# Conditioning products of a two-layer diffusion step: float32 weights stationary on TensorE, the two condition vectors moving

## The chip, the core and the metric

The kernel is one program on one core of a Trainium2 chip. The core has TensorE (matrix products; the profile shows its products as PE and its weight loads as PEld), VectorE (DVE), ScalarE (ACT), GpSimd (POOL), and SyncE (SP), which issues the DMAs. Each engine works through its own list of instructions in order. The metric is the device time of one execution in microseconds; lower is better. Three runs of the kernel before took 1280.70, 1283.64 and 1284.29 us, the median is 1283.64.

## What is computed

One inference step of a network of two layers for 1024 latent tokens and 256 context tokens, 1024 channels, float32. Layer 0 has two attention mixers, layer 1 a Fourier mixer. Ahead of each layer its tokens are normalised, scaled and shifted, and behind it its output is multiplied by a gate. Shift, scale and gate are linear in a conditioning vector; there are two such vectors, `c` for the latent tokens and `c_ctx` for the context. Only these products change. In the reference:

```python
def ada_mod(cvec, w, b):
    m = jax.nn.silu(cvec) @ w + b
    return jnp.split(m, 3, axis=-1)

def modulate(h, shift, scale):
    return h * (1 + scale) + shift
...
    for l in range(DEPTH):
        shc, scc, gtc = ada_mod(c_ctx, ada_w[l], ada_b[l])
        shl, scl, gtl = ada_mod(c, ada_w[l], ada_b[l])
        hc = modulate(rms_norm(xc, norm_g[l]), shc, scc)
        hl = modulate(rms_norm(xl, norm_g[l]), shl[:, None], scl[:, None])
        ...
        xc = xc + gtc * yc
        xl = xl + gtl[:, None] * yl
```

`ada_w[l]` has 1024 rows and 3072 columns: part 0 is the shift, part 1 the scale, part 2 the gate, 1024 columns each. So there are six products, one for each layer and part, of two vectors of 1024 with a matrix of 1024 x 1024.

## The kernel before

Large products run on TensorE in a float32 form (`F32R`) that takes one pass and keeps fewer bits. To keep the precision, an operand is split into a high and a low half (`split`: the high half is a copy, the low half a subtraction), and a product is made of three matmuls, high x high, high x low and low x high (`mm3`, line 249). A matmul's stationary operand is loaded as weights, 128 x 128 at most, and the other operand streams past it.

Buffers come from zones of fixed tiles (`take` and `drop`): `w` has 8 tiles, `p` 4, `pt` 3, `q` 2, `h` 9, `u` 26. A tile is taken again when its last reader is done. The tile framework puts the instructions of each engine in an order of its own when the program is built, so an engine's order isn't that of the code.

The program's stages, with the times of the profiled execution:

- **The first stage** (to 83 us): a fold product (`wa`, line 249), normalising the first 512 tokens, and a loop over 8 chunks `k` of 128 channels. For a chunk, `ada_load` loads two tiles of `ada_w` (parts 0 and 1 of layer 0; 8 blocks of 128 rows by 128 columns, 512 KB), and `ada_chunk` makes shift and scale of these 128 channels. It splits each tile into two halves (lines 261 and 267, on ACT, DVE and POOL) and makes the two condition vectors stationary: `cs4` holds their high and low halves, 4 columns. The tile's halves stream past as 128 columns (lines 491 and 493, `ada`). The result has 4 rows; ACT copies it, and a small plain float32 matmul with `comb` (line 499, `modt`) adds the halves and turns rows into columns. `mod_chunk` makes the modulated chunk, and the projections that need it run (`kv0s`, `kv2s`, `q0s`, `q2s`, line 510).
- **The list `S1`** (83 to 141 us): the other tokens are normalised and modulated (`xt`, line 413, transposes), and keys, values and queries are projected (`kv`, `q`, line 249), normalised, rotated and transposed (`kT`, `qT`, line 646). The letters of `S1` are steps: `n` normalise, `m` modulate, `c` cache, `k`, `q`, `K`, `Q` projections.
- **The attention of mixers A and B** (141 to about 865 us). `soft` makes scores (`sL`, `sC`, line 840) and their exponentials, `weigh` transposes these (`pt`, line 957) and multiplies with the values (`av`, line 963). Between these units a `Filler` runs other work from a queue by cost: projections of the order `ORDER`, and ahead of the first four work items of `qb0`, `qb1` and `g0` the steps named in `COND`: the products (layer 0, part 2), (1, 0) and (1, 1). A step (`Rows.step_ap`) loads 128 rows of a part (512 KB), multiplies them by the first vector's elements and adds on DVE (line 351, two halves), and does the same for the second vector with ACT (line 355) and POOL (line 356). After 8 steps `Rows.finish` splits the two sums and adds their 128 rows with a matmul against ones (line 365), and `row_to_mod` turns the row into columns by 8 small transposes (line 309); the gate's row is stored to memory.
- **Output projection of layer 0** (`oz`), to about 945 us.
- **Layer 1** (from 945 us): gate products (`g1E`, `g1O`, `g1c`), between them the sixth product (1, 2) on DVE alone (`Rows.step`, line 339), the Fourier products and the last projection (`of`).

The lines that the change replaces are 309, 335 to 383 (`Rows`) and 479 to 504.

Of the kernel before, what the change touches and what calls it, by code (L numbers as in the profile page):

```python
# [30 lines left out]
S1 = "c1 n2 m1 c0 m2 K0 Q0 Q2 K2 k6 q8 k4 k8".split()  # L31
E_ML = ("p", "d")
E_MF, E_MH, LC0 = "da", "d", "ppd"
E_AH, E_AL = "a", "dpp"
# [17 lines left out]
COND = ("qb0", "qb1", "g0")  # L52
# [70 lines left out]
def hybrid_step(ctx: ExitStack, tc: tile.TileContext, I, O):  # L123
# [35 lines left out]
    def t_bank(name, dt=F32):  # L159
        return bank("t", name, dt)  # L160
# [34 lines left out]
    cs4 = cp.tile([P, 8, 4], F32R, name="cs4")  # L195
    comb = cp.tile([4, 2], F32, name="comb")
    bT1 = cp.tile([P, 8], F32, name="bT1")
    gT = cp.tile([P, 2, 8], F32, name="gT")
    bT = cp.tile([P, 2, 16], F32, name="bT")
# [17 lines left out]
    dve.tensor_copy(cs4[:, :, 0:2], cs)  # L217
    dve.tensor_sub(cs4[:, :, 2:4], cs, cs4[:, :, 0:2])
    dve.tensor_add(comb, ident[0:4, 0:2], ident[0:4, 2:4])
# [86 lines left out]
    def row_to_mod(l, part, row):  # L306
        tp = t_bank(f"modt{l}{part}")
        for k in range(8):
            pe.transpose(tp[:, 2 * k : 2 * k + 2], row[0:2, k * P : k * P + P], ident[0:2, 0:2])
        tv = tp[:, 0:16].rearrange("p (k v) -> p k v", v=2)  # L310
        bb = bT[:, l, 8 * part : 8 * part + 8].unsqueeze(2).to_broadcast([P, 8, 2])
        if part == 0:
            dve.tensor_add(modb[:, l], tv, bb)
        else:
# [4 lines left out]
    def ada_src(l, part, k):  # L319
        return I["ada_w"][l, k * P : (k + 1) * P, part * D : (part + 1) * D]  # L320

    class Rows:
        def __init__(self, l, part, name, tags):
            self.l, self.part, self.name, self.tags = l, part, name, tags
            self.acc = [take(tags, (P, D)) for v in range(2)]
            for a in self.acc:
                pool.memset(a.a, 0.0)
                if part == 2:
                    sp.dma_start(a[0:1, :], I["ada_b"][l : l + 1, 2 * D : 3 * D])

        def step(self, k, wt=None):
            own = wt is None
            if own:
                wt = take(self.tags, (P, D))
                sp.dma_start(wt.a, ada_src(self.l, self.part, k))
            for v in range(2):
                for h in range(2):
                    sl = slice(h * 512, h * 512 + 512)
                    dve.scalar_tensor_tensor(
                        out=self.acc[v][:, sl], in0=wt[:, sl], scalar=cs[:, k, v : v + 1], in1=self.acc[v][:, sl],  # L340
                        op0=ALU.mult, op1=ALU.add,
                    )
            if own:
                drop(wt)

        def step_ap(self, k):
            wt = take(self.tags, (P, D))
            sp.dma_start(wt.a, ada_src(self.l, self.part, k))
            for h in range(2):
                sl = slice(h * 512, h * 512 + 512)  # L350
                dve.scalar_tensor_tensor(  # L351
                    out=self.acc[0][:, sl], in0=wt[:, sl], scalar=cs[:, k, 0:1], in1=self.acc[0][:, sl],
                    op0=ALU.mult, op1=ALU.add,
                )
            act.activation(wt.a, wt.a, AF.Copy, scale=cs[:, k, 1:2])  # L355
            pool.tensor_add(self.acc[1].a, self.acc[1].a, wt.a)  # L356
            drop(wt)

        def half(self, h, ps, start=True, stop=True):
            for v in range(2):  # L360
                src = self.acc[v][:, h * 512 : h * 512 + 512]
                hi, lo = take("h", (P, 512), F32R), take("h", (P, 512), F32R)
                split(hi.a, lo.a, src)
                for i, part in enumerate((hi, lo)):
                    pe.matmul(
                        ps[0:2, :], ones2[:, v, :], part.a, start=start and v + i == 0, stop=stop and v + i == 2
                    )
                drop(hi, lo)

        def total(self, ps, start=True, stop=True):  # L370
            for h in range(2):
                self.half(h, ps[h], start, stop)
            drop(*self.acc)

        def finish(self, tag):
            row = take(self.tags, (P, D))
            for h in range(2):
                ps = bank(tag, f"{self.name}p{h}")
                self.half(h, ps)
                act.activation(row[0:2, h * 512 : h * 512 + 512], ps[0:2, :], AF.Copy)  # L380
            drop(*self.acc)
            if self.part == 2:
                sp.dma_start(gtd[self.l], row[0:2, :])
            else:
                row_to_mod(self.l, self.part, row.a)
            drop(row)
# [87 lines left out]
    def ada_load(k):  # L474
        out = []
        for part in range(2):
            raw = take(("p", "pt", "q"), (P, 8, P))
            c0 = part * D + k * P
            sp.dma_start(raw.a, I["ada_w"][0, :, c0 : c0 + P].rearrange("(b p) c -> p b c", p=P))
            out.append(raw)  # L480
        return out

    def ada_chunk(k, raws):
        ps = bank("g", f"ada{k}")
        for part, raw in enumerate(raws):
            hi, lo = take("u", (P, 8, P), F32R), take("u", (P, 8, P), F32R)
            split(hi.a, lo.a, raw.a, E_AH, E_AL)
            drop(raw)
            out = ps[0:4, part * P : part * P + P]
            for b in range(8):  # L490
                pe.matmul(out, cs4[:, b, :], hi[:, b, :], start=b == 0, stop=False)
            for b in range(8):
                pe.matmul(out[0:2], cs4[:, b, 0:2], lo[:, b, :], start=False, stop=b == 7)
            drop(hi, lo)
# [3 lines left out]
        for part in range(2):  # L498
            pe.matmul(
                tp[:, 2 * part : 2 * part + 2], row[:, part * P : part * P + P], comb, start=part == 0, stop=part == 1  # L500
            )
        drop(row)
        dve.tensor_scalar(modb[:, 0, k, :], tp[:, 0:2], bT[:, 0, k : k + 1], None, op0=ALU.add)
        dve.tensor_scalar(moda[:, 0, k, :], tp[:, 2:4], bT1[:, k : k + 1], gT[:, 0, k : k + 1], op0=ALU.add, op1=ALU.mult)
# [322 lines left out]
    drop_w(wka)  # L827
    ws["qa1"] = load_w(w0cols(C_QA + 256))
# [181 lines left out]
    cond = dict(zip(COND, ((0, 2), (1, 0), (1, 1))))  # L1010
    rows, wout = {}, []
# [11 lines left out]
    def releaser(nm):  # L1023
        def fn():
            drop_w(ws[nm])
            return 0
        return fn

    def cond_steps(key, ks):
        def fn():  # L1030
            if key not in rows:
                rows[key] = Rows(*key, f"ad{key[0]}{key[1]}", "w")
            for k in ks:
                rows[key].step_ap(k)
            if ks[-1] == 7:
                rows[key].finish("g")
            return 0
        return fn

    for i, nm in enumerate(order):  # L1040
# [302 lines left out]
    r2 = Rows(1, 2, "ad12", BIG)  # L1343
    for c in range(4):
# [43 lines left out]
        for k in ((), (0, 1, 2), (3, 4, 5), (6, 7))[c]:  # L1388
            r2.step(k)
# [4 lines left out]
    r2.finish("g")  # L1394
# [434 lines left out]
```

## Time and profile before

| | us |
|---|---|
| median of 3 runs | 1283.64 |
| the profiled execution | 1282.65 |
| its span, first to last instruction | 1280.9 |
| PE busy in it | 1191.8 |
| DVE / ACT / POOL busy | 955.5 / 639.3 / 489.1 |

The page lists each engine's busy time, then the span in 40 slices of 32 us. A busy PE is not yet PE at its peak: each matmul's record includes its latency, while the next one has already started. What a matmul costs in a stream is the distance from its start to the next one's, its pitch. `PEclk` is the clock that the throttle granted to TensorE, in tenths of full speed. The chain of waits follows the work that ended last back to the start and names TensorE for 62% of the span, DVE for 15%.

### The profile page before, as it was taken

What the parts mean: (1) busy time and instruction counts of PE and PEld (TensorE: products, weight loads), DVE (VectorE), ACT (ScalarE), POOL (GpSimd) and SP (SyncE); (2) the same over time, 40 slices, a digit from 0 to 9 for tenths busy, and PEclk for the clock granted to TensorE, in tenths of its full rate; (3) what the DMA queues carried; (4) which work ended last, traced back from release to release, by engine and by line L of the source; (5) the groups of instructions that cost most, each with busy time, mean ns of one, the idle gap of its engine ahead of it and who ended that gap; (6) DMA issues with size and microseconds to landing.
All of it is one profiled execution on the core that took longest, in us unless ns stands there. A gap on an engine that the chain in (4) does not pass through costs nothing.

```text
span 1280.9 us, 21997 instructions
## 1 busy us (share of the span) xinstructions
PE 1191.8 (93%) x7883; PEld 1066.0 (83%) x7883; DVE 955.5 (75%) x2114; ACT 639.3 (50%) x1239; POOL 489.1 (38%) x386
## 2 busy tenths in 40 slices
PE   5789899999889899999999978889999998999997
PEld 5788899999879798889999977767777888988886
DVE  6789788776987987977887867466874988548553
ACT  5363366565675576756655677431264324333221
POOL 6757665522775754530101042310411215335001
PEclk8898899999999999999999989889999999999999
DMA  9900332324634336344433388596412544346321
GB/s 303 290 6 31 110 90 71 98 68 107 188 110 134 103 122 177 112 138 129 105 90 87 95 241 223 135 253 202 138 59 75 158 154 142 101 140 191 124 90 66
DMA packets 156199, 168.29 MB, mean 131 GB/s; under 512 B 21917, under 2 KB 117161, under 8 KB 156090
## 3 DMA queue, kind: packets, MB, share of 16 engines
q1 hardware_dynamic: 156090, 166.89, 44.4%
q8 instruction: 62, 1.02, 0.4%
q14 instruction: 47, 0.39, 0.1%
HBM read 122.67 MB, written 44.18 MB: 130 GB/s over the span
## 4 chain that ended last, share of the span: by engine, by line
PE 62%; DVE 15%; DMA 11%; issue 5%; POOL 4%; ACT 3%; SPq 1%; POOLq 0%; DVEq 0%; ACTq 0%
PE ga L249 7%; PE of L249 7%; PE av L963 7%; PE pt L957 6%; PE oz L249 5%; PE q L249 4%; PE u L249 4%; PE g1E L249 4%; PE sL L840 3%; PE g1O L249 2%; DVE w L351 2%; PE kv L249 2%; PE sC L840 2%; DVE p L874 2%; DMA od<-e 2%
## 5 line engine op out<-in xcount | busy, mean ns | idle before, releaser
L960 DVE TENSOR_TENSOR pt<-pt,pt 128x512 fp32r<-128x512 f32 (+1 forms) x264 | 171.1, 658 | 34.5 <-ACT pt L261 34.1
L963 PE MATMUL av<-pt,u 128*128 128x256 f32 x1008 | 171.0, 292 | 7.4 <-DVE pt L960 4.0
L261 ACT ACTIVATE pt<-pt 128x512 fp32r<-128x512 f32 (+1 forms) x264 | 146.9, 574 | 60.8 <-PE pt L957 36.4
L957 PE MATMUL pt<-identr,p 128*128 128x128 f32 x1008 | 156.6, 274 | 0.7 <-ACT h L261 0.5
L963 PEld LDWEIGHTS av<-pt,u 128*128 128x128 f32 x1008 | 142.0, 192 | 16.6 <-DVE pt L960 7.1
L267 POOL TENSOR_TENSOR w<-h,w 128x512 fp32r<-128x512 f32 x58 | 79.6, 1384 | 180.6 <-ACT w L261 78.7
L249 PE MATMUL q<-w,u 128*128 128x256 f32 x864 | 132.3, 294 | 1.8 <-DVE u L438 1.0
L957 PEld LDWEIGHTS pt<-identr,p 128*128 128x128 f32 x1008 | 119.7, 141 | 9.5 <-ACT h L261 0.9
L249 PE MATMUL ga<-u,w 128*128 128x512 f32 (+1 forms) x576 | 123.5, 360 | 0.1
L881 ACT ACTIVATE p<-p,nm 128x1280 f32<-128x1280 f32 (+1 forms) x80 | 95.3, 1192 | 54.7 <-DVE p L874 54.3
L249 PEld LDWEIGHTS q<-w,u 128*128 128x128 f32 x864 | 117.1, 195 | 6.1 <-DVE u L438 1.8
L249 PEld LDWEIGHTS ga<-u,w 128*128 128x128 f32 x576 | 93.7, 188 | 15.0 <-ACT pt L261 0.6
L840 PE MATMUL sL<-u,q 128*128 128x512 f32 x256 | 85.2, 418 | 11.6 <-DVE p L874 8.5
L249 PE MATMUL oz<-u,w 128*128 128x512 f32 x240 | 68.5, 413 | 9.8 <-ACT w L261 9.8
L356 POOL TENSOR_TENSOR w<-w,w 128x1024 f32<-128x1024 f32 x24 | 58.6, 2442 | 43.9 <-ACT w L355 33.4
L881 ACT ACTIVATE p<-p,NM 128x640 f32<-128x640 f32 (+2 forms) x80 | 59.2, 740 | 32.4 <-DVE p L874 32.2
L840 PE MATMUL sC<-u,q 128*128 128x256 f32 x320 | 63.2, 300 | 9.4 <-DMA q<-qd 5.8
L249 PE MATMUL of<-u,u 128*128 128x512 f32 (+1 forms) x219 | 65.8, 388 | 0.0
L249 PEld LDWEIGHTS oz<-u,w 128*128 128x128 f32 x240 | 45.9, 196 | 20.0 <-ACT w L261 10.4
L874 DVE TENSOR_SCALAR_CACHE_REDUCE p<-sC,nsink 128x256 f32<-128x256 f32 x80 | 37.8, 475 | 30.3 <-PE sC L840 25.6
L840 PEld LDWEIGHTS sC<-u,q 128*128 128x128 f32 x320 | 48.9, 192 | 13.4 <-issue 5.8
L249 PE MATMUL kv<-w,u 128*128 128x256 f32 x384 | 56.2, 290 | 0.0
(773 smaller groups left out, 2881.8 us busy)
## 6 DMA issues: line engine op xcount, KB each, us to landing
q<-qd SPq DMA_DIRECT2D x80, 256.0 KB
w<-i_ada_w SPq DMA_DIRECT2D x24, 512.0 KB
h<-i_w_in SPq DMA_DIRECT2D x40, 256.0 KB
qd<-h SPq DMA_DIRECT2D x40, 256.0 KB
h<-i_w_out SPq DMA_DIRECT2D x32, 256.0 KB
h<-i_wuT SPq DMA_DIRECT2D x16, 256.0 KB
u<-i_x SPq DMA_DIRECT2D x8, 512.0 KB
p<-i_ada_w SPq DMA_DIRECT2D x8, 512.0 KB
```

Of the source, the lines that this page charges most:

```text
L249: pe.matmul(out, a, b, start=i == 0, stop=i == n - 1)
L261: act.activation(out, in_, AF.Copy)
L267: pick("lo" + lc, lc).tensor_sub(dst_l, src, dst_h)
L351: dve.scalar_tensor_tensor(out=self.acc[0][:, sl], in0=wt[:, sl], scalar=cs[:, k, 0:1], in1=self.acc[0][:, sl], op0=ALU.mult, op1=ALU.add,)
L356: pool.tensor_add(self.acc[1].a, self.acc[1].a, wt.a)
L840: pe.matmul(ps, q[:, s, hc * P : hc * P + P], keys, start=s == 0, stop=s == 1)
L874: dve.tensor_scalar(p[i][:, end[i] : end[i] + n], ps, sign, last[i], op0=ALU.mult, op1=ALU.min, accum_out=c)
L881: act.activation(p[i][:, 0 : end[i]], p[i][:, 0 : end[i]], AF.Exp, bias=last[i], scale=-1.0, accum_out=SU[:, t, hd + i, 0:1],)
L957: pe.transpose(tp[:, jj * 256 + i * P : jj * 256 + i * P + P], p[i][:, off : off + P], ident)
L960: dve.tensor_sub(pt[:, 1, 0:n], tp[:, 0:n], pt[:, 0, 0:n])
L963: pe.matmul(acc, vv, pt[:, s, jj * 256 : jj * 256 + 256], start=c + jj + s == 0, stop=c + jj == nt - 1 and s == 1,)
```

## The change

All six products take one form. A tile of `ada_w` (8 blocks of 128 x 128, as in `ada_load`) is loaded for each chunk of 128 columns, and each block is the stationary operand of a plain float32 matmul, unsplit; the moving operand is `cs`, the two vectors, two columns wide. The result stands as columns already, so the split of the weights, the copy, `comb` and the transposes of shift and scale go. The first layer's shift and scale stay in the loop of the first stage. The other four products, 32 tiles, are put between the steps of `S1` by the table `AT_N`: no tile ahead of the first two steps, two ahead of each of the next four, three ahead of each of four, and four ahead of the last three. The gate's columns become rows by one transpose and are stored at the end of `S1`. `Rows`, `row_to_mod` and the steps of `COND` go.

```diff
+AT_N, AT_Z = (0, 0, 2, 2, 2, 2, 3, 3, 3, 3, 4, 4, 4), ("p", "pt", "q")
-COND = ("qb0", "qb1", "g0")
...
+    def ada_tile(l, part, k, tags):
+        raw = take(tags, (P, 8, P))
+        sp.dma_start(raw.a, ada_src(l, part, k))
+        return raw
+
+    def ada_mm(out, raw, first, last):
+        for b in range(8):
+            pe.matmul(out, raw[:, b, :], cs[:, b, :], start=first and b == 0, stop=last and b == 7)
+        drop(raw)
...
+    def ada_step(l, part, k, raw, tag="g"):
+        if k == 0:
+            acc_ada[l, part] = bank(tag, f"ada{l}{part}")
+        ps = acc_ada[l, part]
+        ada_mm(ps[:, 2 * k : 2 * k + 2], raw, k == 0, k == 7)
+        if k < 7:
+            return
...
     def ada_chunk(k, raws):
         ps = bank("g", f"ada{k}")
         for part, raw in enumerate(raws):
-            hi, lo = take("u", (P, 8, P), F32R), take("u", (P, 8, P), F32R)
-            split(hi.a, lo.a, raw.a, E_AH, E_AL)
-            drop(raw)
-            out = ps[0:4, part * P : part * P + P]
-            for b in range(8):
-                pe.matmul(out, cs4[:, b, :], hi[:, b, :], start=b == 0, stop=False)
-            for b in range(8):
-                pe.matmul(out[0:2], cs4[:, b, 0:2], lo[:, b, :], start=False, stop=b == 7)
-            drop(hi, lo)
-        row = take("e", (4, 256))
-        act.activation(row.a, ps[0:4, 0:256], AF.Copy)
-        tp = t_bank(f"modt{k}")
-        for part in range(2):
-            pe.matmul(
-                tp[:, 2 * part : 2 * part + 2], row[:, part * P : part * P + P], comb, start=part == 0, stop=part == 1
-            )
-        drop(row)
+            ada_mm(ps[:, 2 * part : 2 * part + 2], raw, part == 0, part == 1)
...
+    todo_ada = deque((l, part, k) for l, part in ((0, 2), (1, 0), (1, 1), (1, 2)) for k in range(8))
+
+    def ada_fill(n):
+        for _ in range(min(n, len(todo_ada))):
+            l, part, k = todo_ada.popleft()
+            ada_step(l, part, k, ada_tile(l, part, k, AT_Z), "a")
+
     for n, op in enumerate(S1):
         t = int(op[1])
+        ada_fill(AT_N[n])
...
-        if nm in cond:
-            for n in range(4):
-                cost, fn, key = (*work[n], None)[:3]
-                fl_.add(0.5 * cost, fn, key)
-                fl_.add(0.0, cond_steps(cond[nm], (2 * n,)))
-                fl_.add(0.5 * cost, cond_steps(cond[nm], (2 * n + 1,)))
-            work = work[4:]
...
-        for k in ((), (0, 1, 2), (3, 4, 5), (6, 7))[c]:
-            r2.step(k)
```

Where this puts TensorE's work shows in its order. In a row stands the line, what is written, what it is made from, the stationary rows and the moving columns, and how often. In the first stage of the kernel before, a chunk's products (`ada`) and the small matmul (`modt`) stand among the projections (`kv0s`, `kv2s`, `q2s`):

```order
L510 MATMUL q2s<-w_428,u_500 128x256
L499 MATMUL modt_551<-comb,e_549 128x2 x2
L491 MATMUL ada_563<-u_564,cs_96 4x128 x8
L493 MATMUL ada_563<-u_565,cs_96 2x128 x8
L491 MATMUL ada_563<-u_584,cs_96 4x128 x8
L493 MATMUL ada_563<-u_585,cs_96 2x128 x8
L510 MATMUL kv0s<-w_353,u_499 128x256
L510 MATMUL kv0s<-w_354,u_499 128x256
```

After, the same place has 16 matmuls of a tile's raw blocks for each chunk, and runs of 20 to 23 projections between two chunks:

```order
L446 MATMUL q2s<-w_365,u_310 128x256
L446 MATMUL q2s<-w_366,u_310 128x256
L312 MATMUL ada_416<-cs,p_412 128x2 x8
L312 MATMUL ada_416<-cs,pt_414 128x2 x8
L446 MATMUL kv0s<-w_319,u_407 128x256
L446 MATMUL kv0s<-w_320,u_407 128x256
```

So 32 matmuls of 128 columns and 2 of 2 columns became 16 of 2 columns, with the tile as the weight.

In the list `S1` before, the last projections (`q`) and a transpose of keys (`kT`) lead straight to the first score:

```order
L249 MATMUL q_1828<-w_438,u_1110 128x256
L249 MATMUL q_1828<-w_439,u_1110 128x256
L249 MATMUL q_1828<-w_438,u_1111 128x256
L646 MATMUL kT_1686<-identr,p_1562 128x128 x4
L840 MATMUL sL_0000_1708<-u_1019,q_1701 128x512 x2
```

After, the fourth group of tiles (1, 2) stands there, and the gate row's transpose (`gt`):

```order
L243 MATMUL kv_1670<-w_329,u_997 128x256
L312 MATMUL ada_1508<-cs,p_1506 128x2 x8
L312 MATMUL ada_1508<-cs,pt_1517 128x2 x8
L312 MATMUL ada_1508<-cs,q_1527 128x2 x8
L312 MATMUL ada_1508<-cs,pt_1537 128x2 x8
L582 MATMUL kT_1621<-identr,p_1363 128x128 x4
L312 MATMUL ada_1508<-cs,q_1628 128x2 x8
L312 MATMUL ada_1508<-cs,pt_1638 128x2 x8
L312 MATMUL ada_1508<-cs,p_1648 128x2 x8
L312 MATMUL ada_1508<-cs,pt_1658 128x2 x8
L582 MATMUL qT_1744<-identr,p_1493 128x128 x4
```

The other three groups of 64 are as closed: the first follows a run of 29 projections of `q8`, the third stands after 9 projections and ahead of 87. Ahead of the first score 144 projections of `S1` are done where it were 240; the other 96 follow behind it.

On DVE, in the attention with the filler's `qb0`, before:

```order
L351 SCALAR_TENSOR_TENSOR w_4284<-w_4290,cs,w_4284 128x512 x2
L874 TENSOR_SCALAR p_4120,nm_011_4118<-sC_01_4129,nm_011_4118 128x256
L960 TENSOR_TENSOR pt_4188<-pt_006_4183,pt_4188 128x512
L351 SCALAR_TENSOR_TENSOR w_4284<-w_4296,cs,w_4284 128x512 x2
L960 TENSOR_TENSOR pt_4200<-pt_008_4195,pt_4200 128x512
L874 TENSOR_SCALAR p_4307,nm_000_4305<-sC_00_4308 128x256
```

And after:

```order
L906 TENSOR_TENSOR pt_4312<-pt_006_4307,pt_4312 128x512
L820 TENSOR_SCALAR p_4413,nm_000_4411<-sC_00_4414 128x256
L906 TENSOR_TENSOR pt_4324<-pt_008_4319,pt_4324 128x512
L257 CAST h_4393<-h_4387 128x4x64
L257 CAST h_4396<-h_4387 128x4x64
L820 TENSOR_SCALAR p_4413,nm_001_4412<-sC_00_4414 128x256
```

The two additions over 512 columns between the evictions of scores (line 874) and of transposes (line 960) are gone.

More of the change, by code (lines that the diff above doesn't have):

```diff
@@ new lines, in ada_step, with row_out @@
+        else:
+            col = take("e", (P, 2, 8))
+            dve.tensor_add(col.a.rearrange("p v k -> p k v"), tv, bb)
+            def row_out():
+                tp = t_bank(f"gt{l}")
+                pe.transpose(tp[0:16, 0:P], col.a.rearrange("p v k -> p (v k)"), ident)
+                row = take("e", (16, P))
+                act.activation(row.a, tp[0:16, 0:P], AF.Copy)
+                sp.dma_start(gtd[l].rearrange("v (k c) -> (v k) c", c=P), row.a)
+                drop(col, row)
+            gate_rows.append(row_out)
@@ L474, in ada_load @@
     def ada_load(k):
-        out = []
-        for part in range(2):
[L477 to L481, printed above, removed]
+        return [ada_tile(0, part, k, ("p", "pt", "q")) for part in range(2)]
     def ada_chunk(k, raws):
@@ L827, in hybrid_step @@
     drop_w(wka)
+    for fn in gate_rows:
+        fn()
     ws["qa1"] = load_w(w0cols(C_QA + 256))
```

105 lines of the change are left out of this document (11 added, 94 removed).

## Prediction

> **What bounds the kernel now.** I read the page's head first, then TensorE's busy time by stage, then the chain of waits where TensorE isn't full.
>
> ```profile
> span 1280.9 us, 21997 instructions
> PE 1191.8 (93%) x7883; PEld 1066.0 (83%) x7883; DVE 955.5 (75%) x2114; ACT 639.3 (50%) x1239; POOL 489.1 (38%) x386
> PEclk8898899999999999999999989889999999999999
> ```
>
> The time belongs to TensorE. The table of windows (columns: stretch, its length, then busy us of PE, PEld, DVE, ACT, POOL, the granted clock, DMA) says where it doesn't:
>
> ```profile
> 15.40:85.00 69.60, 56.61 (x511) 52.79 (x510) 55.68 (x69) 35.59 (x54) 46.06 (x26) 0.83 0.70 212
> 83.10:141.00 57.90, 47.39 (x354) 44.88 (x352) 51.60 (x115) 21.94 (x44) 45.75 (x41) 0.88 0.22 66
> 141.00:310.00 169.00, 168.97 (x1331) 162.04 (x1332) 131.88 (x334) 100.85 (x171) 78.73 (x84) 0.99 0.26 74
> 310.00:560.00 250.00, 231.97 (x1695) 209.73 (x1695) 214.97 (x448) 160.15 (x267) 150.22 (x106) 1.00 0.49 142
> 560.00:740.00 180.00, 179.97 (x1216) 165.13 (x1216) 141.93 (x449) 110.83 (x261) 16.22 (x14) 1.00 0.38 100
> ```
>
> In 141 to 310 and 560 to 740 TensorE never rests: there an added matmul costs its full pitch. It waits 18.0 us in 310 to 560 (where the three removed row products run), 13.0 in the first stage and 10.5 in the next. So the question is how many TensorE microseconds the change adds, and which waits they fill.
>
> **The new matmul's price.** No float32 128x128 weight with two moving columns is in the trace, but two neighbours are: L499 (4 rows) and L1600 (1 row), both 128 stationary columns, two moving, plain float32.
>
> ```profile
> L499 PEld LDWEIGHTS modt<-comb,e x32: 181/187/332, 32.1 to 80.6; 4*128 4x128 f32 x32
> ...
> L840 PEld LDWEIGHTS sC<-u,q x320: 186/188/333, 145.7 to 830.8; 128*128 128x128 f32 x160
> ...
> 1140.61 0.96 PEld L1600 LDWEIGHTS pcol<-identr,h 1*128 1x128 f32 x8
> ```
>
> The loop at L499 issues 16 matmuls and the trace holds 32 loads, and L1600's 4 became 8: each float32 product is two load-and-multiply pairs. The eight of L1600 take 0.96 us, so a pair is (0.96 - 0.187)/7 = 0.11 us. Rows don't matter: a load takes a median 187 ns with 4 rows and 188 with 128. So one new product costs **0.22 us** at full clock, about 0.43 at half. There are 384 (48 tiles of 8): 128 in the first stage, 256 before the first score.
>
> The Trainium skill (FP8 and Floating Point Precision, TensorE Precision Notes) says that true FP32 takes four passes through the array. The trace shows two pairs for an instruction, not four; by four such pairs the price would double, which is the third rival.
>
> **The clock decides between 0.22 and 0.43.** The windows below are the 3.41 us steps at which the granted clock changes here; the last two rows are L499's share of two of them.
>
> ```profile
> 42.53:45.95 3.42, 3.42 (x25) 3.18 (x24) 2.48 (x5) 0.88 (x2) 3.06 (x2) 0.50 1.14 326
> 59.60:63.01 3.41, 2.28 (x23) 1.94 (x20) 1.63 (x1) 2.00 (x3) 3.05 (x3) 1.00 0.32 124
> 45.95:49.36 3.41, 3.41 (x22) 3.32 (x21) 3.38 (x2) 2.78 (x3) 3.41 (x3) 0.50 1.07 341
> 63.01:66.43 3.42, 3.42 (x34) 3.42 (x33) 3.35 (x4) 1.86 (x3) 1.91 (x1) 0.50 0.00 0
> 353.15:356.56 3.41, 1.83 (x16) 1.49 (x14) 3.41 (x8) 1.56 (x3) 1.16 (x2) 1.00 0.49 149
> ...
> 42.53:45.95 3.42, 1.01 (x4) 0.92 (x4) 0.40 (x2) 0.50 1.14 326
> 59.60:63.01 3.41, 0.57 (x4) 0.52 (x4) 0.00 (x0) 1.00 0.32 124
> ```
>
> From 42.53 TensorE is occupied without a break at half clock, yet the next window (45.95) is still at half. 63.01 is occupied just as fully and is followed by full clock. The difference is 1.01 us of L499. Falling shows the same: after 59.60 with 2.28 us busy the clock drops, after 353.15 with 1.83 us it stays. Take L499's 0.57 away, and 59.60 has 1.71, the lesser of the two. So time in which TensorE mostly loads weights for two columns does not seem to hold the clock. The new products are nothing else: groups of 64 in a row, 14 us at full clock. I take it that they run at half clock, apart from the first few microseconds of a group. What the rows can't exclude is that L499 fails to count because it has four rows only.
>
> The Trainium skill (TensorE: Matmul & The Clock Gate, Part 1) has the gate open after about 3.4 us of sustained busy time and close after an idle window. Read literally, a stream without gaps would keep full clock; the row at 42.53 speaks against that reading, and it is the first rival.
>
> **A: the first stage (+13).** Before, its products of parts 0 and 1 stream 128 columns past 2 or 4 stationary ones:
>
> ```profile
> 69.45 0.53 PE modt L499 x4
> ...
> 70.55 0.48 PE ada L493 x8
> ...
> 72.51 0.47 PE kv2s L510 x4
> ...
> 278.61 1.31 PE pt L957 x12
> ```
>
> That is 0.06 us each, so a chunk of 32 costs 1.92 + 0.53 = 2.45 us; after, 16 x 0.22 = 3.5 at full, 6.9 at half clock. A projection matmul is 0.118 us, a transpose 0.11.
>
> ```profile
> 7.85 7.55 PE L249 MATMUL wa<-h,w 128*128 128x256 f32 x46 [0.77 <-DVE w L263]
> ...
> 47.27 1.05 PE L510 MATMUL kv2s<-w,u 128*128 128x256 f32 x4
> ...
> 84.88 0.39 PE L510 MATMUL q2s<-w,u 128*128 128x256 f32 x2
> ```
>
> The stage starts at 15.4 and its last projection ended at 85.3, 83.1 without the 20 transposes of the next group that stand between (2.2). After: 128 x 0.43 = 55 us, 192 projections at 0.215 (47.27: four in 0.86 up to the next start) = 41, 32 transposes 7, together 103, so 118 if all at half clock. Off come 3 at the start, 6 for the last 57 projections, which stand alone and regain full clock, and 13 for full windows won by the five runs of 20 projections (4.3 us each holds a whole qualifying window about 3 times in 4: 5 x 0.75 x 3.4). It ends at 96. Ends: 75 at full clock (15.4 + 28 + 23 + 3.5 + 5 waiting), 118 at half. The splits that go (ACT, DVE, POOL) had hidden loads anyway, as the table of DMA shows:
>
> ```profile
> 0.00:60.00 60.00, 41.06 (x328) 37.48 (x328) 43.57 (x53) 27.94 (x41) 39.91 (x28) 0.83 1.02 312
> 60.00:130.00 70.00, 61.04 (x511) 58.05 (x508) 59.92 (x127) 34.24 (x64) 49.68 (x41) 0.90 0.09 29
> ```
>
> The DMA engines are full until 60, so the last tile of part 1 can't land much earlier. From there they are free, and 32 tiles of 0.52 MB at 312 GB/s need 54 us: less than the products that eat them. SP's queue now has these 32 issues among the q stores; each waits for a buffer that a product releases, so the stores stand behind TensorE, and the first load of q behind them.
>
> **B: up to the first score (+97).** 256 x 0.43 = 110. Two of the four groups follow 29 and 87 projections, start at full clock and keep it some 3.8 us (estimate: between none and two windows), which saves 3.7 each: 103. The stage had 10.5 us of waits and 2.2 at its end:
>
> ```profile
> 131.06 7.43 PE L249 MATMUL q<-w,u 128*128 128x256 f32 x48
> ...
> 141.03 0.84 PE L840 MATMUL sL<-u,q 128*128 128x512 f32 x2 [2.23 <-DMA q<-qd]
> ```
>
> The transposes and q8 ahead of the first group keep their waits on DVE; later ones are covered, about 10. Behind a group the projections and the first scores run at half clock until a window fills: +4. DVE's in-order queue now holds the additions that read each group, and waits there; all that stands behind them is wanted only after the next group. 103 - 10 + 4 = 97. The 96 projections that now come after the first score (k4 and one q pair) cost the same there. The two gate rows (a transpose, a copy and a store each) are under 1 us of any engine, and all that reads them comes hundreds of us later. Ends: 107 (no full clock at all), 34 (full clock, 22 us covered, counting also what half clock took).
>
> **C: 310 to 560 (-28).**
>
> ```profile
> L356 POOL TENSOR_TENSOR w<-w,w 128x1024 f32<-128x1024 f32 x24 | 58.6, 2442 | 43.9 <-ACT w L355 33.4 <-issue 8.5 <-DMA w<-i_ada_w 1.9
> L351 DVE SCALAR_TENSOR_TENSOR w<-w,cs,w 128x512 f32<-128x512 f32 x48 | 52.6, 1134 | 4.7 <-DMA w<-i_ada_w 3.9 <-DMA w<-i_ada_b 0.6
> ...
> PE sL L840 <- DVE p L874: 8.5, 7, 1.6
> ...
> L365 PE MATMUL ad02p<-h,ones x8: 391/396/472, 375.4 to 384.4; 128*2 128x512 f32 x8
> ```
>
> 52.6 us of DVE and 58.6 of POOL go. TensorE's longest waits there are for DVE, late by L351; without it the neighbouring stretches show no waits, so 18 us go, and some 3 of latency that a busy time hides after each stop. Three finishes of 8 matmuls with 512 columns (2 x 0.118 = 0.236 each) and 16 transposes go too: 7. Next late there is nothing: TensorE is full. Ends: -31 and -15.
>
> **D: the last row product (-4).**
>
> ```profile
> 987.91 4.42 DMA u<-i_ada_w
> ...
> 992.43 2.74 DVE u L339 x4
> ...
> 1086.78 3.15 PE L249 MATMUL u<-u,u 128*128 128x258 f32 x14 [3.89 <-DVE nyr L1530]
> ```
>
> 8 x 0.236 = 1.9 of TensorE, a wait of 0.5 behind 992.43, and part of the 3.89 us, which DVE owes after a late start on L1429. Ends: -8, -2.
>
> **Sum.** 13 + 97 - 28 - 4 = +78. The profiled execution took 1282.65 (its span and 1.75), the median of the runs is 1 higher: 1360.7, so **1361**. Of this case alone: 1330 to 1392.
>
> **Rivals.**
> 1. The groups keep full clock (0.20). For: they have no gaps and 128 rows. Against: 42.53. A ends at 75 (-8), B is 56 less 11 covered (+45), C and D as above: +5, 1288 (1276 to 1300).
> 2. Faster (0.08): full clock, and the groups stand in waits. A ends at 72 (-11), B 256 x 0.22 = 56 less 22 covered = +34, C -31, D -7: 1268. It decides where B's uncovered part falls below C + D + A's gain, 49. Against it: 64 in a row can't fit between waits of 1 to 3 us.
> 3. A product with 128 rows takes four pairs (0.04): at half clock another 384 x 0.43 = 165, past 1500; at full clock 1288 + 84 = 1372.
> 4. The loads bind (0.04): full clock, but each tile waits for its buffer and then 3 to 5 us of landing, 9 buffers for 32 tiles: some 12 us more than rival 1, 1300.
>
> **Numbers.** The forecast has 0.64. The range 1280 to 1392 holds about 0.95 of it, 0.75 of rival 1, and rival 4: 0.80. A measurement of this kernel can tell 0.3%, 3.9 us, from no change. Faster than 1279.8: rival 2 and a little of 1, 0.10. Within 0.3%: 0.08. Slower: 0.82.
>
> **What would show it.** The clock in the windows of the first 240 us: near 0.5 and the page's first seven PEclk digits at 5 to 7 for the forecast, 8 to 9 for rival 1. L312's records: 768, with a weight load about 0.21 us after the last, or 0.11. The first sL near 240 (before 141), or 167. 310 to 560's counterpart: PE without waits. It would be wrong if streams of weight loads hold the clock, or if the waits of C stay.

## The result, and the profile after

The changed kernel takes **1368.59 us**, the median of 4 runs (1357.95 to 1370.99), against 1282.17 for the kernel before in the same runs: a ratio of 1.066, interval 1.060 to 1.072. The forecast was 1361. Its profiled execution took 1357.95 us, the lowest of the four; its span is 75.2 us longer than before's. All that follows on stages is read from this execution. The other three took 9.5 to 13.0 us longer, and no term of the forecast stands for that.

The head of the page of the changed kernel (span; busy time by engine; granted clock in 40 slices):

```profile
span 1356.1 us, 22633 instructions
PE 1299.0 (96%) x8317; PEld 1185.4 (87%) x8317; DVE 848.2 (63%) x2027; ACT 588.3 (43%) x1169; POOL 359.6 (27%) x328
PEclk7686556999999999999999998988999999999999
```

DVE lost 107 us of work, ACT 51, POOL 130, and TensorE gained 107: the work moved to the engine that bounds the kernel. In the first seven slices the clock is between 5 and 8 tenths, then nearly full. The windows by stage, columns as in the prediction's table (length, busy us of PE, PEld, DVE, ACT, POOL, granted clock, DMA):

```profile
15.40:94.10 78.70, 78.70 (x481) 78.49 (x482) 28.83 (x61) 15.77 (x26) 16.79 (x15) 0.67 0.82 235
94.10:117.20 23.10, 16.30 (x99) 13.94 (x97) 16.59 (x27) 12.53 (x21) 10.68 (x8) 0.78 0.17 46
117.20:234.80 117.60, 117.60 (x652) 117.60 (x651) 28.51 (x74) 8.64 (x19) 18.98 (x22) 0.59 0.43 125
234.80:400.00 165.20, 161.35 (x1256) 153.56 (x1254) 123.88 (x312) 89.04 (x156) 83.97 (x85) 0.98 0.26 75
400.00:640.00 240.00, 238.60 (x1832) 225.67 (x1830) 172.33 (x436) 142.12 (x249) 70.22 (x70) 1.00 0.34 97
```

The third row holds the four groups of products: TensorE has no idle time in it and runs at a clock of 0.59. The last row is the attention that had 18.0 us of waits before; it has 1.4 left. Where the stages end now, from the timeline (start, duration, operation):

```profile
93.37 0.87 PE L446 MATMUL q2s<-w,u 128*128 128x256 f32 x6
...
234.80 1.20 PE L786 MATMUL sL<-u,q 128*128 128x512 f32 x2
```

The first stage ends at 94.1 (forecast 96, before 83.1 without the transposes), the first score stands at 234.8 (forecast near 240, before 141.0). Since 96 projections now follow the first score, the two programs are better compared where the same work is done. These are the last keys and values, the last gate product of the attention and the Nyquist column `pn` in layer 1. Before (instructions of a tile: count, ns, first and last start):

```profile
L249 PE MATMUL kv<-w,u x384: 274/281/415, 101.8 to 310.1; 128*128 128x256 f32 x192
L249 PE MATMUL ga<-u,w x576: 274/392/502, 498.6 to 739.8; 128*128 128x512 f32 x128, 128*128 128x256 f32 x64
L1555 PE MATMUL pn<-u,nyq x12: 275/278/281, 1135.1 to 1136.8; 128*4 128x256 f32 x12
```

After:

```profile
L243 PE MATMUL kv<-w,u x384: 276/281/562, 172.6 to 420.2; 128*128 128x256 f32 x192
L243 PE MATMUL ga<-u,w x576: 275/392/489, 589.1 to 822.7; 128*128 128x512 f32 x128, 128*128 128x256 f32 x64
L1478 PE MATMUL pn<-u,nyq x12: 276/279/281, 1210.4 to 1212.1; 128*4 128x256 f32 x12
```

The distance between the two is 11.0 us at the end of the first stage, 110.1 at the last keys, 82.9 at the last gate product, 75.3 at `pn` and 75.2 at the end. So the four terms of the forecast came out like this:

| term | forecast | measured |
|---|---|---|
| A, first stage | +13 | +11.0 |
| B, up to the steady scores | +97 | +99.1 |
| C, attention without row products | -28 | -27.2 |
| D, the last row product | -4 | -7.7 |
| sum | +78 | +75.2 |

### The profile page after: what moved, and what is told of

Its sections match the earlier page's. It is cut to its first block, busy times and chain, and to the rows that moved or that the text cites. A ratio compares the mean times of both kernels' runs of the same rounds, so it can differ in the third digit from the quotient of the medians.

```text
span 1356.1 us, 22633 instructions
## 1 busy us (share of the span) xinstructions
PE 1299.0 (96%) x8317; PEld 1185.4 (87%) x8317; DVE 848.2 (63%) x2027; ACT 588.3 (43%) x1169; POOL 359.6 (27%) x328
## 4 chain that ended last, share of the span: by engine, by line
PE 79%; DMA 10%; DVE 5%; issue 2%; ACT 2%; POOL 1%; SPq 1%; POOLq 0%; DVEq 0%; ACTq 0%
PE ada L312 10%; PE ga L243 8%; PE av L909 7%; PE of L243 7%; PE q L243 7%; PE pt L903 6%; PE oz L243 4%; PE u L243 4%; PE sL L786 4%; PE kv L243 3%; PE g1E L243 3%; PE g1O L243 3%; PE sC L786 2%; PE g1c L243 2%; DMA q<-qd 2%
## 5 line engine op out<-in xcount | busy, mean ns | idle before, releaser
L909 PEld LDWEIGHTS av<-pt,u 128*128 128x128 f32 x1008 | 140.1, 191 | 15.8 <-DVE e L920 7.6
L243 PE MATMUL ga<-u,w 128*128 128x512 f32 (+1 forms) x576 | 126.7, 362 | 0.4 <-DVE h L712 0.4
L243 PEld LDWEIGHTS ga<-u,w 128*128 128x128 f32 x576 | 94.1, 189 | 14.5 <-issue 0.8
L243 PE MATMUL of<-u,u 128*128 128x512 f32 (+1 forms) x173 | 55.4, 387 | 0.0
L312 PEld LDWEIGHTS ada<-cs,p 128*128 128x128 f32 x304 | 54.1, 278 | 0.4 <-DMA p<-i_ada_w 0.2
L312 PE MATMUL ada<-cs,p 128*128 128x2 f32 x304 | 54.1, 311 | 0.0
```

The source lines that it names most:

```text
L243: pe.matmul(out, a, b, start=i == 0, stop=i == n - 1)
L312: pe.matmul(out, raw[:, b, :], cs[:, b, :], start=first and b == 0, stop=last and b == 7)
L909: pe.matmul(acc, vv, pt[:, s, jj * 256 : jj * 256 + 256], start=c + jj + s == 0, stop=c + jj == nt - 1 and s == 1,)
```

## Experiments

Theory: streams of weight loads for two columns don't hold TensorE's clock, so the products run at half clock, and their time on TensorE is the loss. Rivals: the half clock comes from something else; the price isn't one of the clock; the 32 loads or the order of the new program set the pace.

### Adding work that streams columns

If the theory is right, added matmuls that only stream columns raise the clock. Each of the 32 later tiles got such matmuls between its products:

```
         h, _ = wka[0]
         for b in range(8):
             pe.matmul(
                 ps[:, 2 * k : 2 * k + 2], raw[:, b, :], cs[:, b, :], start=k == 0 and b == 0, stop=k == 7 and b == 7
             )
+            for _ in range(3 - b % 2 * 3):
+                pe.matmul(ps[:, 16:512], h[:, 3, 0:P], h[:, 0:2, 0:248], start=False, stop=False)
```

> The changed kernel, plus 12 matmuls of 496 streamed columns for each of the 32 later tiles (384 in all, three behind every second product; their sums land in unused columns and nobody reads them, so this is added work only). At full clock each takes about 0.23 us (0.236 for 512 columns in the profile before). Theory (weight loading for two columns does not hold the clock, streamed columns do): the groups run at full clock, a tile takes 8 x 0.22 + 12 x 0.23 = 4.5 us, 144 us where the changed kernel's groups took 98; so only +40 to +50 us over the changed kernel's profiled 1358 for 88 us of added streaming: 1398 to 1408, the products' pitch at 0.11 us a pair and the granted clock in the groups near 1. Rival 1 (the groups run at half clock for another reason): 384 x 0.46 = +176, 1534. Rival 2 (a product costs 0.43 us at any clock): +88, 1446.

Measured: 1410.87 us, ratio 1.100 (1.096 to 1.103), 42 us above the changed kernel for 384 added matmuls; that is 3 us above the end of my range. The stretch of the four groups, and one place in it (timeline):

```profile
121.40:279.20 157.80, 157.80 (x1030) 143.97 (x1028) 28.17 (x73) 8.21 (x18) 19.22 (x22) 1.00 0.33 93
```

```profile
150.34 0.50 PE L323 MATMUL ada<-cs,p 128*128 128x2 f32 x4
150.70 0.93 PE L327 MATMUL ada<-w 128*128 128x496 f32 x3
151.47 0.50 PE L323 MATMUL ada<-cs,p 128*128 128x2 f32 x4
```

The clock is 1.00 throughout, and the same products now take full-clock time: a round of four pairs and three streaming matmuls lasts 1.13 us (150.34 to 151.47), of which three times 0.226 (the median pitch of these matmuls) is streamed. The four pairs have 0.45, 0.11 each, where they took 0.21 in the changed kernel. Rival 1 (1534) and rival 2 (1446) are out.

The next pair asks how much streaming it takes; only the number in `range` differs, so that two or eight matmuls are added to a tile.

> The kernel with added streaming matmuls, but two of 496 columns for each later tile (64 in all) in place of twelve; nobody reads their sums. Theory (windows of 3.4 us in which less than about a third of the time streams columns lose the clock): 2 x 0.226 of 2.2 us is a fifth, so the groups run at half clock as in the changed kernel and the added work costs its half-clock price, 64 x 0.46 = +29 over the changed kernel, 1385 to 1400. Rival (any streaming between the loads keeps the clock): 2.2 us a tile, 70 for 98, 1335 to 1345.

> The same with eight for each later tile (256 in all). Theory: 8 x 0.226 of 3.4 us is a little over half, above the third at which the clock falls in the other runs and below the 0.7 that it takes to come back; the first group starts at full clock, so it stays: 32 x 3.4 = 109 us of groups, +11 over the changed kernel's 98, and 4 less behind them: 1373 to 1385, so faster than with two although four times as much is added. Rival (half of the time isn't enough): half clock, 32 x 6.9 = 220, 1485 to 1495.

Measured: 1394.42 (ratio 1.090, 1.084 to 1.095) with two, **1378.23** (1.075, 1.073 to 1.078) with eight. The groups with two, then with eight:

```profile
120.20:258.30 138.10, 138.10 (x706) 133.56 (x705) 28.42 (x73) 8.22 (x18) 19.00 (x22) 0.59 0.36 106
```

```profile
123.40:252.50 129.10, 129.10 (x898) 119.68 (x897) 28.19 (x73) 8.22 (x18) 19.22 (x22) 1.00 0.40 114
```

Four times as much added work is 16 us faster. Two matmuls leave the clock at 0.59 and cost 26 us, 0.40 each, near their half-clock price of 0.46; eight hold it at 1.00. Being occupied isn't what counts, since TensorE is occupied without a break in both. Both times lie in their ranges. But the shares of streaming on which these two expectations rest, a third and 0.7, are not fixed by them: the runs say only that about a fifth is too little and that about half is enough once the clock is full.

### Where the products stand, and which operand moves

Two kernels do all products of the later parts, one tile at a time in a bank of its own, so that they stand among the projections:

```
-        ps = acc_ada[l, part]
-        ada_mm(ps[:, 2 * k : 2 * k + 2], raw, k == 0, k == 7)
+        tp = t_bank(f"ada{l}{part}{k}")
+        ada_mm(tp[:, 0:2], raw, True, True)
```

> The changed kernel with a bank of its own for each of the 32 later tiles, so that the products of a tile stand where their tile is issued, 8 to 32 in a row between projections and transposes, and not 64 in a row. Products unchanged. Theory (clock by the share of streamed columns in a window of 3.4 us): part of the products now shares its windows with projections; between all at full clock (256 x 0.22 - 11 of covered waits = +45) and all at half (+97): I take +75, so 1283 + 11 + 75 - 35 = 1334. Rival (half clock belongs to the products wherever they stand): as the changed kernel, 1358 to 1370.

Measured: 1359.19, ratio 1.061 (1.057 to 1.065); the interval overlaps that of the changed kernel. My 1334 was wrong and the rival's range held. The stretch with the products:

```profile
110.50:227.60 117.10, 117.10 (x670) 116.50 (x670) 43.16 (x131) 13.35 (x29) 27.06 (x29) 0.62 0.47 133
```

The clock is 0.62. In TensorE's order the pairs still stand in runs of 16 to 112, and TensorE is occupied without a break. I take it that the projections between the runs are too few; this run alone doesn't show that. It doesn't prove either that half clock belongs to the products wherever they stand; the runs with added streaming show the contrary.

The second exchanges the operands as well. The vectors become the stationary operand and the weights stream:

```
+        for b in range(8):
+            pe.matmul(ps[0:2, 0:P], cs[:, b, :], raw[:, b, :], start=b == 0, stop=b == 7)
+        row = take("e", (2, P))
+        act.activation(row.a, ps[0:2, 0:P], AF.Copy)
...
+        pe.transpose(tp[:, 0:2], row.a, ident[0:2, 0:2])
```

> As the kernel with a bank for each tile, but with the operands of each later product exchanged: the two vectors are the stationary operand (128 rows, two columns) and the raw float32 weights move, 128 columns in each product; each tile's row of 128 is copied by ACT and transposed (32 more transposes of 0.1 us). Theory (streamed columns hold the clock, weight loads do not): full clock; a product takes between 0.11 us (a plain float32 transpose of 128 columns in the profile before) and 0.22: 1283 + 11 + (28 + 3 - 11 or 56 + 3 - 11) - 35 = 1279 to 1307. Rival (the clock falls with plain float32 products whatever moves): half clock, 0.43 a product, within 10 us of the kernel with a bank for each tile.

Measured: 1320.68, ratio 1.031 (1.026 to 1.035): 38.5 us less than with the tile as the weight, 14 above my range. The stretch, and one tile:

```profile
110.00:211.50 101.50, 99.92 (x795) 78.04 (x796) 49.06 (x146) 22.98 (x61) 33.14 (x34) 0.98 0.58 159
```

```profile
147.59 1.91 PE L320 MATMUL ada<-p,cs 128*2 128x128 f32 x16
```

The clock is 0.98. A tile of 8 products (16 pairs) takes (1.91 - 0.27) / 15 = 0.11 us a pair, so at full clock a product costs 0.22 us in either arrangement. What differs on TensorE, apart from one small transpose for each tile, is whether the time goes to loading or to streaming. The range was missed at two places: the first stage, which has its weights stationary still, ended at 97.3 here and not at 94, and B was +58 where I had 48.

### The loads

> The changed kernel without seven of the eight products of each of the 32 later tiles; all loads, buffers and additions stay. So the later parts' vectors are not the reference's. Theory (the products themselves are the cost, the loads are not): 32 products of 0.22 to 0.43 = 7 to 14 us, which fall into waits; the first stage keeps its +11, the attention stage its -28, the last row product its -7: 1283 - 24 + 0 to 6, so 1258 to 1265, faster than before. Rival (loads, buffers or queues bind in this stage): above 1283, and TensorE waits for tiles that land.

The edit:

```
-        ada_mm(ps[:, 2 * k : 2 * k + 2], raw, k == 0, k == 7)
+        pe.matmul(ps[:, 2 * k : 2 * k + 2], raw[:, 0, :], cs[:, 0, :], start=k == 0, stop=k == 7)
+        drop(raw)
```

Measured: 1309.82, ratio 1.021 (1.017 to 1.026). The theory as I had put it here falls: with seven eighths of the products gone, the kernel is still 2% slower than before. The stretch ahead of the first score, and TensorE's waits from there into the scores (what waited for what, us in total, times, longest):

```profile
99.00:182.00 83.00, 58.27 (x396) 54.16 (x394) 45.29 (x102) 21.13 (x40) 31.15 (x31) 0.77 0.70 189
```

```profile
PE qT L583 <- POOL h L578: 6.6, 1, 6.6
PE sL L787 <- DVE p L821: 5.2, 2, 4.9
PE ada L321 <- DMA pt<-i_ada_w: 4.9, 3, 3.6
```

TensorE idles 24.7 of 83.0 us and runs at 0.77. Is it the loads, or the order of the new program? As many products, 32, were made from four loaded tiles, one for each later part. The table `AT_N` changes with them, so that each of the four tiles stands ahead of a step of its own:

```
-AT_N, AT_Z = (0, 0, 2, 2, 2, 2, 3, 3, 3, 3, 4, 4, 4), ("p", "pt", "q")
+AT_N, AT_Z = (0, 0, 0, 1, 0, 1, 0, 1, 1, 0, 0, 0, 0), ("p", "pt", "q")
...
-        ada_mm(ps[:, 2 * k : 2 * k + 2], raw, k == 0, k == 7)
+        for j in range(8):
+            pe.matmul(ps[:, 2 * j : 2 * j + 2], raw[:, j, :], cs[:, j, :], start=j == 0, stop=j == 7)
+        drop(raw)
...
-    todo_ada = deque((l, part, k) for l, part in ((0, 2), (1, 0), (1, 1), (1, 2)) for k in range(8))
+    todo_ada = deque((l, part, k) for l, part in ((0, 2), (1, 0), (1, 1), (1, 2)) for k in range(1))
```

> As many products as in the kernel with one of eight (32 in all), but from only four loaded tiles, one for each later part, so that 28 loads of 0.52 MB go; the later parts' vectors are not the reference's. Theory (in the kernel with one of eight the loads set the pace, which the full set of products covers): TensorE's 36 us of waits between the first stage and the steady scores fall to about 12, 1283 + 16 - 28 - 7 + 7 = 1271, so 1262 to 1280. Rival (what is left over there comes from the order of the changed program, not from the loads): 1300 to 1310, as with 32 loads.

Measured: 1280.47 (10 runs), ratio 0.996 (0.992 to 0.999), 29 us less than with 32 loads and at the upper end of the range. Its profiled execution, from which the rows below come, was the fastest of the ten (1270.18). From the end of the first stage to the first score, and the two rows to compare with those above:

```profile
94.80:156.30 61.50, 53.09 (x372) 50.34 (x371) 49.15 (x110) 20.40 (x42) 34.82 (x33) 0.81 0.19 60
```

```profile
L243 PE MATMUL kv<-w,u x384: 274/281/580, 131.1 to 330.3; 128*128 128x256 f32 x192
L243 PE MATMUL ga<-u,w x576: 276/392/483, 498.6 to 733.6; 128*128 128x512 f32 x128, 128*128 128x256 f32 x64
```

So the loads, with the buffers that they hold, cost some 30 us in this stage when hardly any products cover them: 29 in the medians (33 by the two ratios to the kernel before), and 30 in the profiles: from the end of the first stage to the last keys the kernel with one of eight takes 38.8 us longer than the kernel before, and this one 8.5. Only 9.7 us of TensorE's waits with 32 loads name the landing of a tile; how much of the rest goes through the buffers, and how much through the place of the tiles in the program, these two runs don't separate. In the changed kernel TensorE has no idle time among the groups, so the products hide the loads there. The kernel with four tiles also gives a cleaner reading of the attention than the changed one: it is 20.2 us behind the kernel before at the last keys and 6.2 ahead at the last gate product. C is worth 26.4 without the groups; its span, 1267.9 for 1280.9, leaves 6.8 for D.

### The first stage

Only the first stage put back to split weights (`ada_chunk`, `cs4`, `comb` as before):

> The changed kernel with the first stage's products done as before (split weights moving, four columns stationary); the later parts stay as changed. Theory (the first stage costs 11 to 18 us and the rest is its own): 1368.6 less 11 to 18, so 1351 to 1358. Rival (the first stage's clock or its late end costs the next stage too): 1345 or less.

Measured: 1359.91, ratio 1.057 (1.050 to 1.065), 2 us above my range. The interval overlaps that of the changed kernel, so this run alone settles little. Its trace tells where most of the 11 us of the first stage go. The four groups (PE's product time and clock):

```profile
107.20:132.45 25.25, 25.21 (x128) 0.54 0.37 104
135.00:162.20 27.20, 27.20 (x128) 0.50 0.55 162
165.80:193.00 27.20, 27.18 (x128) 0.50 0.47 142
205.70:230.90 25.20, 24.81 (x128) 0.55 0.32 89
```

They take 104.4 us, in the changed kernel 97.6: they begin with less full clock. At the last keys this execution is 3.2 us ahead of the changed kernel's (417.0 for 420.2). It still ends 7.4 later (span 1363.5 for 1356.1): behind the last gate product it loses 10.9, at a lower granted clock, for which the change gives no reason.

Now the first stage alone with its operands exchanged, on the kernel before and on the changed kernel (there with the exchange in the later parts as well):

```
-            for b in range(8):
-                pe.matmul(out, cs4[:, b, :], hi[:, b, :], start=b == 0, stop=False)
...
+            for b in range(8):
+                pe.matmul(
+                    ps[0:2, part * P : part * P + P], cs[:, b, :], raw[:, b, :],
+                    start=part + b == 0, stop=part == 1 and b == 7,
+                )
```

> The kernel before, with the first stage's products alone exchanged: the two vectors stationary, raw float32 weights moving, no splits; the later parts as before. Theory (a product costs 0.22 us at full clock, streamed columns hold the clock): 28 us of products, 23 of projections, 7 of transposes and waits from 15.4 on; loads last until 60; the stage ends between 75 and 83 where before it ended at 83: 1274 to 1282. Rival (plain float32 products bring half clock here too): it ends at 94 or later, 1294 or more.

> The changed kernel with the operands exchanged in both stages: two vectors stationary, raw float32 weights moving, 128 columns a product. Theory (the clock stays up in the first stage too): the kernel with later products exchanged (1320.7) less its first stage's 16 and up to 8 more: 1296 to 1305. Rival (the first stage is set by something else than the clock): 1315 or more.

Measured: **1277.36** (10 runs; ratio 0.994, 0.991 to 0.997) for the first, 1297.61 (10 runs; 1.010, 1.006 to 1.014) for the second, both in the theory's ranges; the kernel before took 1284.78 beside them. The first stage of the first:

```profile
15.40:78.90 63.50, 60.71 (x511) 50.41 (x510) 31.31 (x64) 22.25 (x40) 19.10 (x17) 1.00 0.81 232
```

The clock is 1.00, although these products take more TensorE time at full clock (3.5 us a chunk) than the split ones (2.45). It is the only kernel of the study that does the whole computation and is faster than the kernel before, by 0.6%: the first stage's products on TensorE with raw weights that move, and the later row products left where they were.

### A second profile

> The changed kernel once more, unchanged, for a second profile: the profiled execution took 1357.95 us, the three others 1367.5 to 1371.0. Theory (the program is the same, but where the 3.4 us steps of the clock fall differs between executions; the first stage and the four groups are where this matters): if this execution takes 1365 or more, the first stage ends 3 to 7 us later than at 94.1 and the groups sum to 101 to 106 instead of 97.6, and from the steady scores on the two profiles run alike within 2 us. Rival (the difference lies elsewhere): both stages as in the first profile, and the distance grows in the attention or in layer 1.

The profiled execution took 1357.70, so the condition wasn't met; the other took 1367.7. The two profiles differ by 2.2 us at the end of the first stage and by 0.1 at the last keys. Why other executions take some 10 us longer is not settled. It isn't that the kept ones are always fast: in the kernel with the first stage as before, the kept execution was the slowest of four (1365.32). The clock has a part in it: the mean granted clock was 0.927 in both kept executions of the changed kernel and 0.919 to 0.926 in the four others. As an estimate from spans and clocks, the share of time that is not granted grows by 2 to 12 us of the 9 to 13, in three of the four by more than half of the distance. In which stage that happens no trace shows.

## Why the forecast held, step by step

**The price.** Right. The first three rows of the loads of `ada` (min, median, max ns) hold 304 + 256 + 208 = 768 loads for 384 products, two pairs each:

```profile
L312 PEld LDWEIGHTS ada<-cs,p x304: 186/333/338, 15.4 to 230.0; 128*128 128x128 f32 x152
L312 PEld LDWEIGHTS ada<-cs,pt x256: 187/333/339, 17.2 to 233.4; 128*128 128x128 f32 x128
L312 PEld LDWEIGHTS ada<-cs,q x208: 186/333/337, 22.1 to 223.2; 128*128 128x128 f32 x104
```

Rival 3, four pairs to a product, is refuted by the count.

**The clock.** Right, but for one digit: of the first seven of the page, six are 5 to 7 and one is 8. The doubt about four rows is settled too: these products have 128. The start of the first group in the steps of the clock, with L312's time alone (length, PE, PEld, clock):

```profile
117.25:120.66 3.41, 3.41 (x33) 3.41 (x32) 1.00 0.11 35
120.66:124.07 3.41, 3.41 (x19) 3.41 (x18) 0.50 0.41 124
124.07:127.49 3.42, 3.42 (x18) 3.42 (x18) 0.50 0.00 0
```

A step filled with products to the last is followed by half clock, and it stays there, for all 27.1 us of the second group below. The Trainium skill (TensorE: Matmul & The Clock Gate, Part 1) has the gate open after about 3.4 us of sustained busy time. This trace does not agree: the busy time of these products does not open it. The runs with two and with eight added matmuls show it beside each other (0.59 and 1.00, both without a gap).

**A, +13 for +11.0.** The stage is occupied without a break, as forecast, and ended 2 us earlier. That it came so close is in part luck: a mean clock of 0.67 over 78.7 us means about 27 us at full clock, where the forecast's 3, 6 and 13 make 22, and its 118 at half clock were some 3 us too few. In the eight other profiles of this study with the same first stage its end lies between 94.8 and 101.0, so this one is the earliest of nine.

**B, +97 for +99.1.** The sum is near because errors cancel. The groups, L312's time alone:

```profile
117.20:141.20 24.00, 24.00 (x128) 23.97 (x128) 0.57 0.39 111
144.00:171.10 27.10, 27.10 (x128) 27.10 (x128) 0.50 0.54 160
174.70:198.80 24.10, 24.10 (x128) 24.09 (x128) 0.57 0.53 162
210.90:233.71 22.81, 22.42 (x128) 22.38 (x128) 0.62 0.37 99
```

They take 97.6 where I had 103: three groups, not two, begin with some full clock.

The larger error is in the waits. I took about 10 us of covered waits off, nearly all of the 10.5 that TensorE waited from 83.1 to 141. But 5.6 of these stand at the transposes `xt` and at projections up to 101 us, ahead of the place of the first group, and by my own sentence those stay. Only 4.9 stood where a group could cover them: the wait of 2.23 before the first score, which the prediction shows, and three before the transposes `qT`:

```profile
121.73 0.53 PE L646 MATMUL qT<-identr,h 128*128 128x128 f32 x4 [0.94 <-POOL h L641]
129.67 0.54 PE L646 MATMUL qT<-identr,q 128*128 128x128 f32 x4 [1.26 <-POOL q L641]
130.71 0.51 PE L646 MATMUL qT<-identr,q 128*128 128x128 f32 x4 [0.50 <-DVE q L641]
```

These did go: from 117.2 to 234.8 TensorE has no idle time. But it waits 6.8 us ahead of the first group now, and 3.9 from 234.8 to 400, behind the groups, most of it at three places, where the kernel before waited 0.03 in all from 141 to 310:

```profile
249.00 4.53 PE L243 MATMUL q<-w,u 128*128 128x256 f32 x36 [1.17 <-ACT h L610]
276.53 0.35 PE L909 MATMUL av<-pt,u 128*128 128x256 f32 x1 [1.20 <-DVE e L920]
277.44 1.05 PE L909 MATMUL av<-pt,u 128*128 128x256 f32 x4 [0.56 <-DVE pt L906]
```

Together that is 10.7 for 10.5: in sum nothing came off. It leaves 99.1 - 97.6 - 0.2 = 1.3 us for what half clock costs the work between and behind the groups, where I had 4. So the errors are -5, +10 and -3.

**C, -28 for -27.2.** Right, by the step that was given: DVE no longer late, and nothing late in its place (1.4 us of waits in 400 to 640). Between the last keys and the last gate product, before and after:

```profile
310.10:739.80 429.70, 411.64 (x2908) 374.56 (x2907) 356.90 (x897) 270.79 (x527) 166.34 (x120) 1.00 0.44 124
420.20:822.70 402.50, 400.25 (x2887) 372.38 (x2886) 299.47 (x848) 241.62 (x489) 83.42 (x80) 1.00 0.36 101
```

TensorE's waits fall by 15.8 us, where I had 18, and its busy time by 11.4, where I had 10 (7 of matmuls and 3 of latency; no row shows the latency by itself). The kernel with four tiles has the whole at 26.4.

**D, -4 for -7.7.** Mis-sized, near the end of its range. Between the first `u` product of layer 1 and `pn`, 65.1 us before became 58.6; the finish's TensorE work (1.9) and the whole wait of 3.9 went, where I had counted only a part of the wait. The other 1.9 of the 7.7 is not traced.

**Rival 1**, full clock in the groups, was refuted by the clock. Its price of 1288 was probably too low as well: the kernel with both exchanges, the nearest to it that was run, has a clock of 0.97 and 1.00 in the two stages at the same 0.22 a product, and takes 1297.6. At the last keys it has +58 for B where rival 1 had +45; I had taken 11 us of covered waits off there too. **Rival 4**, that the loads bind at full clock, found no support there: in the kernel with the later products exchanged TensorE idles 1.6 of the 101.5 us shown above. In these runs the loads show, with some 30 us, where most of the products are gone.

## What to carry to other kernels

Before giving TensorE a product with a wide weight and few moving columns, ask which operand moves: the time may be the same on paper (0.22 us here), but here loading weights let the granted clock fall to half and streaming them kept it full. That repairs the clock, not the place of the work: with both stages exchanged the kernel is still 1% slower than before, because the products of the later parts stand on the engine that bounds it. What a moved piece of work costs on the bounding engine is its time at the clock that it will bring about, less only those waits that lie where it will stand. And when a cost is taken away by experiment, look at what it had covered: without most of the products, the loads showed.

## What the runs showed of the hardware that was not expected

Added work can be faster than less added work: eight useless matmuls a tile took 16 us less than two. At full clock a plain float32 product is two pairs of 0.11 us whichever operand is the vectors, 128 columns loaded with two moving or two loaded with 128 moving. And executions of one program took 1357.7 and 1357.95 us, where a trace was kept, and 1367.5 to 1371.0 where none was, at a mean granted clock of 0.927 and of 0.919 to 0.926; no run here tells why.
